# The MLP's up products of an encoder step: pairs of weight blocks multiplied in seven block products instead of eight, each accumulator in a tile of its own, and the norm's rate squared and applied at the down products

## The chip, the cores and the metric

One Trainium2 chip, of which the kernel uses one core. The metric is the device time of one execution in microseconds (us). Before the change it is 2514.52 us, the median of three runs (2514.13 to 2517.27).

## What is computed

The reference is one step of a two-layer encoder on 640 tokens with 1024 features, in float32. The part that the change touches is the end of each layer:

```python
x = x + mix @ w_o
h2 = rmsnorm(x, ln2)
x = x + jnp.square(jax.nn.relu(h2 @ w_up)) @ w_down
```

`w_up` is 1024 x 4096 and `w_down` 4096 x 1024. `rmsnorm` multiplies each token by one number, its rate (the reciprocal root of the mean square), and each feature by a weight of `ln2`. The rate is positive, so `relu(rate * v)**2` is `rate**2 * relu(v)**2`.

## The kernel before, in words

**Layout.** Activations lie with the features on the 128 partitions, so a [1024, 640] activation is a tile of 8 chunks (`k`) of 640 tokens. Tokens are cut in two halves of 320 (`half[0]`, `half[1]`; `HT` is 320). A weight block is 128 output columns by all 1024 inputs, one [128, 1024] tile of 512 KB: `w_up` has 32 blocks, `w_down` 4 x 8.

**Precision.** Every operand is split in two numbers of lower precision, `hi` and `lo` (`split`, lines 132 to 134: ScalarE copies `hi`, then VectorE subtracts to get `lo`). A product is three matmuls, `hi*hi`, `hi*lo` and `lo*hi` (`three`, lines 185 to 194, issued through `mm`, line 80). In the order of a block these are the weight's `hi` with the activation's `hi`, the weight's `hi` with its `lo`, and the weight's `lo` with its `hi`: the third matmul of a block is the first that needs the weight's `lo`. A block is 2 halves x 8 chunks x 3 = 48 matmuls of 128 x 320.

**Weights.** `Feed` (line 136) loads the blocks in a fixed order: `raw` has three buffers, and a load (line 146, on SyncE's queue) starts when the block three places back has been read for the last time. `whi` and `wlo` have two buffers each. `ahead` splits the next block while the one before is in use. The split can only start when TensorE has finished the block that had the buffer before, two places back; with 48 matmuls in each block there is one whole block of time for it. Splits are given priority over other work of their engines by `AHEAD`.

**The MLP** (`mlp`, line 1097). The 4096 inner features come in four groups `b` of 8 blocks. `up(b, ms)` multiplies blocks; `relu2` (lines 1106 to 1111) turns each PSUM result into `gh`, `gl`: VectorE takes relu and rate in one instruction (L1108), ScalarE squares to `gh` (L1109), GpSimd squares again in full precision (L1110), VectorE subtracts for `gl` (L1111). The order is: all of up 0; then for each `b` two blocks of up `b+1`, the 8 blocks of down `b`, and the other six of up `b+1`. A down block is added to `x` by VectorE (L1131, and L1058 in the last group, inside `residual`, which also starts the next norm). TensorE's order is the order of the code; on the other engines a scheduler with priorities orders the instructions.

**PSUM** has eight banks of 512 columns: two pairs `g` (`pair`, line 182) that the blocks take in turn, and two banks each with the tags `c` and `d` (`bank`, line 179).

**The norm before the MLP** is folded in: `residual_raw` (line 1072) makes `Ah`, `Al` from `x * ln2` without the rate while the last product of the attention part runs; `Norm.rate` (line 305) makes the rate beside the first up block, into the tile `nrm.r`.

Of the kernel before, what the change touches and what calls it, by code (L numbers as in the profile page):

```python
# [9 lines left out]
F32 = mybir.dt.float32  # L10
F32R = mybir.dt.float32r
AF = mybir.ActivationFunctionType
ALU = mybir.AluOpType
# [49 lines left out]
def encoder(ctx, tc, xin, wblk, wba, sct, sdelta, prow, pcol, gates, wst, bsr, convw, consts, delta0,  # L63
# [72 lines left out]
    class Feed:  # L136
# [143 lines left out]
    class Norm:  # L280
        def __init__(self, pl, c0, nm, final=False, whole=False):
            self.pl, self.c0, self.nm, self.final = pl, c0, nm, final
            self.r = pl.tile([P, NT], F32, tag="rate", name=f"rate{nm}") if whole else None
            self.acc = pl.tile([P, 2, HT], F32, tag="acc", name=f"acc{nm}")
# [20 lines left out]
        def rate(self, a, wait=3):  # L305
# [21 lines left out]
            nc.scalar.activation(u, pr[:, 0:HT], AF.Copy)  # L327
# [490 lines left out]
    def heads(l, ond, msd, gd, close, norm):  # L818
# [4 lines left out]
        with phase(f"first{l}", 1) as pf:  # L823
# [9 lines left out]
            else:  # L833

                nrm = Norm(pf, 0, "a", whole=True)
# [114 lines left out]
    def merge(l, ond, msd, gd):  # L950
        with phase(f"merge{l}", 1) as pl:
# [99 lines left out]
            es = ExitStack()  # L1051
            nrm = Norm(es.enter_context(phase(f"nb{l}", side="right")), 8 * (2 * l + 1), f"b{l}", whole=True)
            return es, nrm, residual_raw(l, WB_WO, Bh, Bl, f"wo{l}", nrm)

    def residual(l, b0, ah, al, nm, nrm):

        def add(xs, ps, dst, first):
            nc.vector.tensor_tensor(xs, ps[:, :, 0:HT], xs, op=ALU.add)  # L1058
            nrm.add(dst, xs, first, nc.vector if dst == 1 else nc.gpsimd)

        for m in range(4):
            run(gemm(l, b0 + m, ah, al, f"{nm}{m}", lambda ps: add(v2(x[:, m, :]), ps, None, m == 0)))
        with phase(f"g{nm}") as pw:
            g = group(l, range(b0 + 4, b0 + 8), ah, al, nm,
                      lambda i, a, ps: add(x[:, 4 + 2 * i:6 + 2 * i, half[a]], ps, a, False), pw)
            for _ in range(16):
                next(g)
            run(g, fin := nrm.finish(0))
            run(fin)
        return nrm.finish(1)  # L1070
# [26 lines left out]
    def mlp(l, es, nrm, rates):  # L1097
        with phase(f"mlp{l}", 5) as pl:
# [6 lines left out]

            def relu2(ps, hi, lo):
                r = pl.tile([P, 2, HT], F32, tag="r", bufs=3, name=f"r{l}")
                nc.vector.scalar_tensor_tensor(r[:], ps[:, :, 0:HT], 0.0, v2(nrm.r[:]), op0=ALU.max, op1=ALU.mult)  # L1108
                nc.scalar.activation(hi, r[:], AF.Square)  # L1109
                nc.gpsimd.tensor_tensor(r[:], r[:], r[:], op=ALU.mult)  # L1110
                nc.vector.tensor_tensor(lo, r[:], hi.bitcast(F32), op=ALU.subtract)  # L1111
# [6 lines left out]
            up(0, range(KC))  # L1118
            for b in range(FF // D):
                if b + 1 < FF // D:  # L1120
                    up(b + 1, range(2))
                gh, gl = Chunks(tiles, b, 0), Chunks(tiles, b, 1)
                if b + 1 == FF // D:
                    last = l + 1 == DEPTH
                    es.close()
                    es = ExitStack()
                    pn = es.enter_context(phase(f"na{l}", side="right"))
                    return es.close, residual(l, WB_DN + b * KC, gh, gl, f"dn{l}", Norm(pn, 32 if last else 16 * (l + 1), f"a{l}", last))
                for m in range(KC):
                    def add(ps):  # L1130
                        nc.vector.tensor_tensor(v2(x[:, m, :]), ps[:, :, 0:HT], v2(x[:, m, :]), op=ALU.add)  # L1131
                    run(gemm(l, WB_DN + b * KC + m, gh, gl, f"dn{l}{b}{m}", add))
                up(b + 1, range(2, KC))
# [109 lines left out]
```

## Time and profile before

| what | value |
|---|---|
| median of three runs | 2514.52 us |
| the profiled execution's own time | 2513.98 us |
| its span, first to last instruction | 2512.3 us |
| TensorE matmul busy | 2464.4 us (98%) |
| TensorE weight load busy | 2387.2 us (95%) |
| VectorE busy | 1300.4 us (52%) |
| ScalarE busy | 1026.6 us (41%) |
| GpSimd busy | 568.3 us (23%) |
| mean granted TensorE clock | 0.994 |
| up and down products of layer 0 | from 800.5 to about 1261 us |
| up and down products of layer 1 | from about 2040 to 2497 us |

The profile is one execution. PE is TensorE's matmul, PEld its weight load, DVE VectorE, ACT ScalarE, POOL GpSimd, SP SyncE, whose queue issues the loads. A matmul's record lasts longer than the distance to the next one, because matmuls are pipelined: the distance is what counts. Lines such as L133 are lines of the kernel; `whi<-raw` means output `whi`, input `raw`.

### The profile page before, as it was taken

To read this page: it belongs to the slowest core of one execution; us is meant where nothing else is said; L and a number is where in the kernel's file an instruction comes from. 1 tells how busy PE (TensorE), PEld (TensorE's weight loads), DVE (VectorE), ACT (ScalarE), POOL (GpSimd) and SP (SyncE) were. 2 spreads that over 40 slices of the span, in tenths; PEclk is the share of its full clock that TensorE was granted. 3 is DMA by queue.
4 is the path that set the end of the run, shared out by engine and by line. 5 is a ranking of instruction groups with operands and counts; after the bars stand their busy time and mean duration, and the time that the engine had idled before them with its cause. 6 is when DMAs were issued, how large, how long until landed. Compare 5 with 4: busy or idle time off the path is not lost. (4 is left out here: it accounts for less than half of the span.)

```text
span 2512.3 us, 45051 instructions
## 1 busy us (share of the span) xinstructions
PE 2464.4 (98%) x18456; PEld 2387.2 (95%) x18456; DVE 1300.4 (52%) x2686; ACT 1026.6 (41%) x1968; POOL 568.3 (23%) x638
## 2 busy tenths in 40 slices
PE   8999999999999999999999999999999999999998
PEld 7999999998999999999999999999989999999997
DVE  6656776527455433333346677664275553333333
ACT  5767666533123212122347676774322222122122
POOL 0233433211222201011213343331112221011012
PEclk9999999999999999999999999999999999999999
DMA  5233333346532222222233333343564322222221
GB/s 175 83 107 122 103 96 99 115 132 228 167 95 74 72 75 74 76 76 76 85 94 115 102 96 96 101 127 113 164 204 145 92 68 76 76 76 76 73 71 67
DMA packets 124493, 261.28 MB, mean 104 GB/s; under 512 B 17232, under 2 KB 57072, under 8 KB 124288
## 3 DMA queue, kind: packets, MB, share of 16 engines
q1 hardware_dynamic: 123968, 257.10, 32.3%
q8 instruction: 145, 2.38, 0.4%
q0 software_dynamic: 320, 1.31, 0.2%
q14 instruction: 60, 0.49, 0.1%
HBM read 218.22 MB, written 40.15 MB: 103 GB/s over the span
## 5 line engine op out<-in xcount | busy, mean ns | idle before, releaser
L133 ACT ACTIVATE whi<-raw 128x1024 fp32r<-128x1024 f32 x304 | 321.8, 1059 | 1003.9 <-issue 369.6
L134 DVE TENSOR_TENSOR wlo<-raw,whi 128x1024 fp32r<-128x1024 f32 x304 | 397.8, 1309 | 167.8 <-ACT whi L133 153.6
L80 PE MATMUL pg_dn<-gl,whi 128*128 128x320 f32 x1024 | 316.6, 309 | 2.1 <-DVE gl L1111 2.1
L80 PE MATMUL pg_up<-Ah,whi 128*128 128x320 f32 x1024 | 317.1, 310 | 0.0
L80 PE MATMUL pg_dn<-gh,whi 128*128 128x320 f32 x1024 | 316.8, 309 | 0.0
L80 PE MATMUL pg_up<-Ah,wlo 128*128 128x320 f32 x1024 | 316.4, 309 | 0.0
L80 PE MATMUL pg_dn<-gh,wlo 128*128 128x320 f32 x1024 | 316.4, 309 | 0.0
L80 PE MATMUL pg_up<-Al,whi 128*128 128x320 f32 x1024 | 316.4, 309 | 0.0
L80 PE MATMUL pg_g<-Ah,whi 128*128 128x320 f32 x896 | 289.4, 323 | 1.3 <-ACT sg L821 1.3
L80 PE MATMUL pg_g<-Ah,wlo 128*128 128x320 f32 x896 | 276.9, 309 | 0.1
L80 PE MATMUL pg_g<-Al,whi 128*128 128x320 f32 x896 | 276.4, 308 | 0.0
L1110 POOL TENSOR_TENSOR r<-r 128x640 f32<-128x640 f32 x64 | 101.8, 1590 | 684.8 <-ACT gh L1109 684.8
L80 PE MATMUL pg_p<-Ah,whi 128*128 128x320 f32 x768 | 251.4, 327 | 0.0
L80 PE MATMUL pg_p<-Al,whi 128*128 128x320 f32 x768 | 237.0, 309 | 0.4 <-DVE Al L134 0.4
L80 PE MATMUL pg_p<-Ah,wlo 128*128 128x320 f32 x768 | 237.3, 309 | 0.0
L80 PEld LDWEIGHTS pg_dn<-gl,whi 128*128 128x128 f32 x1024 | 192.2, 188 | 2.6 <-DVE gl L1111 2.6
L80 PEld LDWEIGHTS pg_up<-Ah,whi 128*128 128x128 f32 x1024 | 192.2, 188 | 0.0
L80 PEld LDWEIGHTS pg_up<-Al,whi 128*128 128x128 f32 x1024 | 192.2, 188 | 0.0
L80 PEld LDWEIGHTS pg_dn<-gh,whi 128*128 128x128 f32 x1024 | 192.2, 188 | 0.0
L80 PEld LDWEIGHTS pg_dn<-gh,wlo 128*128 128x128 f32 x1024 | 192.2, 188 | 0.0
L80 PEld LDWEIGHTS pg_up<-Ah,wlo 128*128 128x128 f32 x1024 | 192.2, 188 | 0.0
L80 PEld LDWEIGHTS pg_g<-Ah,whi 128*128 128x128 f32 x896 | 168.6, 188 | 9.0 <-issue 3.5
(689 smaller groups left out, 5394.5 us busy)
## 6 DMA issues: line engine op xcount, KB each, us to landing
raw<-in_wblk SPq DMA_DIRECT2D x304, 512.0 KB, 3.6
gd<-sg SPq DMA_DIRECT2D x56, 320.0 KB, 3.5
rg<-gd SPq DMA_DIRECT2D x44, 320.0 KB, 3.3
S<-in_sdelta SPq DMA_DIRECT2D x16, 512.0 KB, 5.7
out<-S SPq DMA_DIRECT2D x16, 512.0 KB, 3.8
gr<-rowd SPq DMA_DIRECT2D x16, 320.0 KB, 5.0
er<-rowd SPq DMA_DIRECT2D x16, 320.0 KB, 4.0
ond<-osb SPq DMA_DIRECT2D x16, 320.0 KB, 2.2
```

Source lines behind the costliest of these rows:

```text
L80: nc.tensor.matmul(out, lhsT=lhsT, rhs=rhs, start=start, stop=stop, **kw)
L133: nc.scalar.activation(dst_hi, src, AF.Copy)
L134: nc.vector.tensor_tensor(dst_lo, src, dst_hi.bitcast(F32), op=ALU.subtract)
L1110: nc.gpsimd.tensor_tensor(r[:], r[:], r[:], op=ALU.mult)
```

## The change

Two neighbouring up blocks, the two halves of the 1024 inputs and the two token halves make a 2 x 2 by 2 x 2 product of blocks: eight products of 12 matmuls (4 chunks x 3). The change computes it in seven, by an identity of the Strassen-Winograd kind.

- `A[k, a]` are the four quarters of the activation (input half `k`, token half `a`). Four sums of them are made once a layer in full precision and split: `S1`, `S2` and `S4` into new tiles, `S3` in place of `A[0, 1]` in `Ah`, `Al`. That takes 16 scaled copies on ScalarE (`scaled`), four sums on VectorE (`plus`) and four splits of 4 x 320 columns. They lie among the first four up blocks of a layer, which are still multiplied the old way.
- `B[k, i]` are the quarters of the two weight blocks (input half `k`, block `i`). Four combinations of them (`s1`, `s2`, 512 columns each) are made by VectorE for each pair, before they are split.
- `seven(b, m)` multiplies blocks `m` and `m+1`. Its weight tiles are `wa` (first raw block: two products), `wb` (the two of `s1`: two products), `wc` (one of `s2` and a quarter of the second raw block: two products) and `wd` (512 columns, the other of `s2`: one product). They take the two buffers of `whi` and `wlo` in turn.
- The accumulators are `Z` (bank `c`), `X` (bank `d`) and `Y` (one bank of a pair). `Z` and `X` are read in the middle of their accumulation (`z1`, `z2`, `x5` are ScalarE copies), and go on accumulating after the read.
- There are 14 such pairs in a layer (two in group 0, four in each of the others), 28 in all. 336 matmuls fewer are issued, which is 28 x 12.
- The rate is no longer applied in the up blocks: `nrm.r` holds its square, and each down block is multiplied by it on VectorE before it is added to `x`, two instructions of 640 columns in place of one (`plus_products`; `residual` takes it as an argument).
- Relu goes to ScalarE. In `seven` ScalarE takes both squares; GpSimd has no instruction there.
- The order of groups stays: pairs `(0, 4)`, `(0, 6)`, `(1, 0)`, eight down blocks, `(1, 2)`, `(1, 4)`, `(1, 6)`, `(2, 0)`, eight down blocks, and so on.

The core of the diff (`Norm` also takes another pool for the rate tile, and `merge` returns three pools instead of one):

```diff
         def parts(self, pl):
-            raw = self.raw.pop(0)
+            self.last = self.raw.pop(0)
+            return self.of(pl, self.last[:])
+
+        def of(self, pl, *src):
             hi = pl.tile([P, D], F32R, tag="whi", bufs=2, name="whi")
             lo = pl.tile([P, D], F32R, tag="wlo", bufs=2, name="wlo")
+            at = 0
             with tc.high_priority(offset=AHEAD):
-                split(hi[:], lo[:], raw[:])
+                for v in src:
+                    n = v.shape[-1]
+                    split(hi[:, at:at + n], lo[:, at:at + n], v)
+                    at += n
             return hi, lo
...
-            nc.scalar.activation(u, pr[:, 0:HT], AF.Copy)
+            nc.scalar.activation(u, pr[:, 0:HT], AF.Copy if self.power == 1 else AF.Square)
...
         def add(xs, ps, dst, first):
-            nc.vector.tensor_tensor(xs, ps[:, :, 0:HT], xs, op=ALU.add)
+            plus(xs, ps, dst)
...
+            def squares(r, hi, lo, eng):
+                nc.scalar.activation(hi, r, AF.Square)
+                if eng is None:
+                    nc.scalar.activation(r, r, AF.Square)
+                else:
+                    eng.tensor_tensor(r, r, r, op=ALU.mult)
+                nc.vector.tensor_tensor(lo, r, hi.bitcast(F32), op=ALU.subtract)
...
             def relu2(ps, hi, lo):
-                r = pl.tile([P, 2, HT], F32, tag="r", bufs=3, name=f"r{l}")
-                nc.vector.scalar_tensor_tensor(r[:], ps[:, :, 0:HT], 0.0, v2(nrm.r[:]), op0=ALU.max, op1=ALU.mult)
-                nc.scalar.activation(hi, r[:], AF.Square)
-                nc.gpsimd.tensor_tensor(r[:], r[:], r[:], op=ALU.mult)
-                nc.vector.tensor_tensor(lo, r[:], hi.bitcast(F32), op=ALU.subtract)
+                r = flat("r", 2)
+                nc.scalar.activation(r[:], ps[:, :, 0:HT], AF.Relu)
+                squares(r[:], hi, lo, nc.gpsimd)
...
-            up(0, range(KC))
+            q, p, sm, u, v = tmp
+            up(0, range(1))
+            scaled(q, 1, 1)
+            scaled(p, 0, 1)
+            plus(sm, p, q)
+            split(*S[1], sm)
+            up(0, range(1, 2))
+            scaled(u, 0, 0)
+            plus(sm, sm, u)
+            split(*S[2], sm)
+            plus(p, p, u)
+            scaled(v, 1, 0)
+            up(0, range(2, 3))
+            plus(sm, sm, v)
+            split(*S[4], sm)
+            up(0, range(3, 4))
+            split(*S[3], p)
...
+            def seven(b, m):
+                gh, gl = dst(b, m)
+                wa = feed.take(l, WB_UP + b * KC + m, ahead=False)
...
+                s1, s2 = (pt.tile([P, 2, 512], F32, tag=t, name=f"{t}{l}{b}{m}") for t in ("t1", "t2"))
+                with tc.high_priority(offset=AHEAD):
...
+                    sub(s1[:, 1, :], B[0, 0], B[0, 1])
+                    neg(s1[:, 0, :], s1[:, 1, :], B[1, 1])
+                wb = feed.of(wp, s1[:].rearrange("p a b -> p (a b)"))
+                Z, X = (bank(t, f"{n}{l}{b}{m}")[:, 0:HT] for n, t in ("zc", "xd"))
+                Y = pair(f"y{l}{b}{m}")[:, 0, 0:HT]
...
+                product(Z, wa, 0, A[0, 0], True)
+                z1 = copy("z1", Z)
+                product(Y, wa, 1, A[1, 0], True)
+                r0, r1 = flat("ra", 2), flat("rb", 2)
+                add(r0[:, 0, :], Y, z1)
+                with tc.high_priority(offset=AHEAD):
+                    sub(s2[:, 0, :], B[1, 1], B[0, 1])
+                    neg(s2[:, 1, :], s1[:, 0, :], B[1, 0])
+                wc = feed.of(wp, s2[:, 0, :], B[1, 1])
+                feed.load()
+                product(Z, wb, 0, S[2], False)
+                z2 = copy("z2", Z)
+                product(X, wb, 1, S[1], True)
+                x5 = copy("x5", X)
+                wd = feed.of(wp, s2[:, 1, :])
+                product(Z, wc, 0, S[3], False)
+                with tc.high_priority(offset=AHEAD):
+                    add(r1[:, 1, :], Z, x5)
+                product(X, wc, 1, S[4], False)
+                add(r0[:, 1, :], X, z2)
+                nc.scalar.activation(r0[:], r0[:], AF.Relu)
+                squares(r0[:], gh[:, :, half[0]], gl[:, :, half[0]], None)
+                feed.ahead()
+                product(Z, wd, 0, A[1, 1], False)
+                nc.scalar.activation(r1[:, 0, :], Z, AF.Relu, scale=-1.0)
+                nc.scalar.activation(r1[:, 1, :], r1[:, 1, :], AF.Relu, scale=-1.0)
+                squares(r1[:], gh[:, :, half[1]], gl[:, :, half[1]], None)
+
+            def plus_products(xs, ps, a):
+                t = flat("t", 2)
+                rate = v2(nrm.r[:]) if a is None else rep(nrm.r[:, half[a]], 1, 2)
+                nc.vector.tensor_tensor(t[:], ps[:, :, 0:HT], rate, op=ALU.mult)
+                nc.vector.tensor_tensor(xs, t[:], xs, op=ALU.add)
```

In the orders below, the changed kernel's L1199 is a matmul of a product, L1204 the copies `z1`, `z2`, `x5`, L1208 the sums with them, L1185 and L1186 the combinations of weights, L1230, L1234 and L1235 relu, L1123 and L1125 the two squares, L1128 the subtraction for `gl`; L133, L134 are the split in both kernels.

ScalarE from the end of one pair to the middle of the next, layer 0. Before, two up blocks there:

```order
L133 ACTIVATE whi<-raw_94_9252 128x1024
L1109 ACTIVATE gh_9308<-r_9365 128x640
L133 ACTIVATE whi<-raw_95_9314 128x1024
L1109 ACTIVATE gh_9308<-r_9425 128x640
L133 ACTIVATE whi<-raw_96_9374 128x1024
```

Now, from the split of the next pair's `wa` (`raw_96`; `t_9633` is the next pair's `s1`, `t_9634` its `s2`, `ra`, `rb` the results of the two token halves):

```order
L133 ACTIVATE whi<-raw_96_9475 128x1024
L1230 ACTIVATE ra_9533<-ra_9533 128x640
L1123 ACTIVATE gh_9494<-ra_9533 128x2x320
L133 ACTIVATE whi<-t_9633 128x1024
L1125 ACTIVATE ra_9533<-ra_9533 128x640
L1234 ACTIVATE rb_9534<-ps_z_9504 128x320
L1204 ACTIVATE z_9656<-ps_z_9641 128x320
L1123 ACTIVATE gh_9494<-rb_9534 128x2x320
L1125 ACTIVATE rb_9534<-rb_9534 128x640
L133 ACTIVATE whi<-t_9634 128x512
L133 ACTIVATE whi<-raw_97_9544 128x512
L1204 ACTIVATE z_9695<-ps_z_9641 128x320
```

Relu and both squares of the pair that ends now stand between the splits of the next pair's first three weight tiles, and the copies of the accumulators stand behind them.

VectorE in the same place. Before, two up blocks:

```order
L1108 SCALAR_TENSOR_TENSOR r_9365<-pg_up_9316,rateb_8518 128x640
L134 TENSOR_TENSOR wlo<-raw_94_9252,whi 128x1024
L1111 TENSOR_TENSOR gl_9309<-r_9365,gh_9308 128x640
L1108 SCALAR_TENSOR_TENSOR r_9425<-pg_up_9376,rateb_8518 128x640
L134 TENSOR_TENSOR wlo<-raw_95_9314,whi 128x1024
```

Now, from the `lo` of a pair's `wa` on:

```order
L134 TENSOR_TENSOR wlo<-raw_94_9295,whi 128x1024
L134 TENSOR_TENSOR wlo<-t_9496,whi 128x1024
L1128 TENSOR_TENSOR gl_9358<-ra_9396,gh_9357 128x2x320
L1208 TENSOR_TENSOR ra_9533<-pg_y_9506,z_9519 128x320
L1185 TENSOR_TENSOR t_9633<-raw_96_9475,raw_97_9544 128x512
L134 TENSOR_TENSOR wlo<-t_9497,whi 128x512
L134 TENSOR_TENSOR wlo<-raw_95_9407,whi 128x512
L1186 SCALAR_TENSOR_TENSOR t_9633<-t_9633,raw_97_9544 128x512
L1128 TENSOR_TENSOR gl_9358<-rb_9397,gh_9357 128x2x320
L134 TENSOR_TENSOR wlo<-t_9497,whi 128x512
L1185 TENSOR_TENSOR t_9634<-raw_97_9544 128x512
L1208 TENSOR_TENSOR rb_9534<-ps_z_9504,x_9572 128x320
```

After these two more stand before the next `wa`: the last combination (L1186, 512 columns) and the sum with `X` (L1208). So there are 14 instructions to a pair where two blocks had six; the combination of the pair after (`t_9633`) stands ahead of the split of this pair's `wc`.

ScalarE at the first pair of a layer, where the sums of activations are split (`S2h`, `S4h`, and `Ah<-s_9049`, which is `S3`; `raw_91` to `raw_93` are blocks 3 to 5; `t_9359` is the first pair's `s1`). Before:

```order
L133 ACTIVATE whi<-raw_91_9042 128x1024
L1109 ACTIVATE gh_9036<-r_9181 128x640
L133 ACTIVATE whi<-raw_92_9130 128x1024
L1109 ACTIVATE gh_9186<-r_9243 128x640
L133 ACTIVATE whi<-raw_93_9192 128x1024
```

Now:

```order
L133 ACTIVATE whi<-raw_92_9158 128x1024
L133 ACTIVATE S2h_9044<-s_9050 128x1280
L1132 ACTIVATE r_9283<-pg_up_9234 128x640
L1123 ACTIVATE gh_9226<-r_9283 128x640
L133 ACTIVATE Ah<-s_9049 128x4x320
L133 ACTIVATE S4h_9046<-s_9050 128x1280
L133 ACTIVATE whi<-t_9359 128x1024
L1132 ACTIVATE r_9346<-pg_up_9297 128x640
L1204 ACTIVATE z_9382<-ps_z_9367 128x320
```

The split of `wb` and the first copy of an accumulator stand behind `S3` and `S4`; `S3` overwrites a part of `Ah` and so waits for the fourth up block's last matmul.

More of the change, by code (lines that the diff above doesn't have):

```diff
@@ L280, in encoder, with __init__ @@
     class Norm:
-        def __init__(self, pl, c0, nm, final=False, whole=False):
-            self.pl, self.c0, self.nm, self.final = pl, c0, nm, final
-            self.r = pl.tile([P, NT], F32, tag="rate", name=f"rate{nm}") if whole else None
+        def __init__(self, pl, c0, nm, final=False, whole=None, power=1):
+            self.pl, self.c0, self.nm, self.final, self.power = pl, c0, nm, final, power
+            self.r = whole.tile([P, NT], F32, tag="rate", name=f"rate{nm}") if whole else None
             self.acc = pl.tile([P, 2, HT], F32, tag="acc", name=f"acc{nm}")
@@ L1116, in up @@
                     run(gemm(l, WB_UP + b * KC + m, Ah, Al, f"up{l}{b}{m}", lambda ps: relu2(ps, hi, lo)), rates)
-            up(0, range(KC))
+            A = {(k, a): [v[:, 4 * k:4 * k + 4, half[a]] for v in (Ah, Al)] for k in range(2) for a in range(2)}
+            S = {i: [psum_pool.tile([P, 4, HT], F32R, name=f"S{i}{t}{l}")[:] for t in "hl"] for i in (1, 2, 4)}
+            S[3] = A[0, 1]
+            tmp = [pl.tile([P, 4, HT], F32, tag=t, name=f"s{i}{l}")[:] for i, t in enumerate(("gh", "gl", "gh", "gl", "gh"))]
@@ new lines, in scaled, with plus @@
+            def scaled(d, k, a):
+                for i in range(4):
+                    c = nrm.c0 + 4 * k + i
+                    nc.scalar.activation(d[:, i, :], x[:, 4 * k + i, half[a]], AF.Copy, scale=col[:, c:c + 1])
+            def plus(d, s0, s1):
+                nc.vector.tensor_tensor(d, s0, s1, op=ALU.add)
+            q, p, sm, u, v = tmp
[4 more added lines that the diff above has]
+            split(*S[1], sm)
@@ L1124, in mlp @@
                     last = l + 1 == DEPTH
-                    es.close()
-                    es = ExitStack()
+                    stacks.pop().close()
+                    stacks.pop().close()
+                    es = stacks.pop()
                     pn = es.enter_context(phase(f"na{l}", side="right"))
-                    return es.close, residual(l, WB_DN + b * KC, gh, gl, f"dn{l}", Norm(pn, 32 if last else 16 * (l + 1), f"a{l}", last))
+                    return es.close, residual(l, WB_DN + b * KC, gh, gl, f"dn{l}", Norm(pn, 32 if last else 16 * (l + 1), f"a{l}", last), plus_products)
                 for m in range(KC):
[L1130 to L1133, printed above, removed]
+                    run(gemm(l, WB_DN + b * KC + m, gh, gl, f"dn{l}{b}{m}", lambda ps: plus_products(v2(x[:, m, :]), ps, None)))
+                for m in (2, 4, 6):
+                    seven(b + 1, m)
     ctx.enter_context(tc.manual_schedule(engines={mybir.EngineType.PE}))
```

41 lines of the change are left out of this document (34 added, 7 removed).

## The prediction

> **What bounds the kernel now.** I read the page first, then the stretches of one layer's MLP, then TensorE's waits. The page's first part gives the shares:
>
> ```profile
> span 2512.3 us, 45051 instructions
> PE 2464.4 (98%) x18456; PEld 2387.2 (95%) x18456; DVE 1300.4 (52%) x2686; ACT 1026.6 (41%) x1968; POOL 568.3 (23%) x638
> ```
>
> TensorE bounds it: busy for 98%. The table by stretches, here one inside the MLP (busy time and count of matmul, weight load, VectorE, ScalarE, GpSimd, then the granted clock), gives the price of a matmul:
>
> ```profile
> 880.00:1000.00 120.00, 120.00 (x820) 120.00 (x819) 41.47 (x42) 23.18 (x25) 12.69 (x8) 1.00 0.24 76
> ```
>
> 820 matmuls in 120 us are 0.1463 us each. A block of 48 takes 7.02, a block product of 12 takes 1.756. VectorE is busy there for 35% and ScalarE for 19%, so they have room, but what counts is when each of their pieces ends. What TensorE waits for now, in the whole run (total, times, longest):
>
> ```profile
> PE pg_pb L80 <- DVE mix L1036: 9.7, 2, 4.9
> ...
> PE ps_msa L80 <- DVE acca L303: 4.5, 2, 2.9
> ...
> PE pg_dn L80 <- DVE gl L1111: 2.1, 2, 1.1
> PE ps_mrb L80 <- DVE dgb L317: 1.9, 2, 1.0
> ```
>
> Inside the MLPs only the last two and a part of the second lie. So fewer matmuls are time, and every new wait of TensorE is time too.
>
> **The change: matmuls removed.** 336 x 0.1463 = 49.2 us. Nothing else on TensorE is added. The border of two blocks costs nothing today (the timeline below has the distance 0.15 across it), so I take the same for a product that starts on another accumulator.
>
> **The change: a wait at the end of each pair.** The next weight tile (`wa` of the next pair, or the first down block) takes the buffer of `wc`, and between `wc` and it lies only `wd`, one product. Before, a whole block of 7.02 lay there. How long a split takes from the release of the buffer is seen at the border from an up to a down block (start, duration, engine):
>
> ```profile
> 987.39 0.31 PE L80 MATMUL pg_dn<-gh,whi 128*128 128x320 f32 x1
> ...
> 987.49 1.06 ACT L133 ACTIVATE whi<-raw 128x1024 fp32r<-128x1024 f32 x1 [5.34 <-issue]
> ...
> 987.59 0.82 DVE L1108 SCALAR_TENSOR_TENSOR r<-pg_up,rateb 128x640 f32<-128x640 f32 x1 [2.85 <-PE pg_up L80]
> ...
> 988.58 1.23 DVE L134 TENSOR_TENSOR wlo<-raw,whi 128x1024 fp32r<-128x1024 f32 x1 [0.17 <-ACT whi L133]
> ```
>
> ScalarE starts 0.10 after the next block's first matmul, takes 1.06, VectorE follows after 0.03 and takes 1.23. What TensorE then needs is seen where it waits for VectorE:
>
> ```profile
> 1201.67 0.31 PE L80 MATMUL pg_dn<-gh,whi 128*128 128x320 f32 x1
> ...
> 1202.15 0.82 DVE L1111 TENSOR_TENSOR gl<-r,gh 128x640 fp32r<-128x640 f32 x1 [1.14 <-POOL r L1110]
> ...
> 1203.03 0.41 PE L80 MATMUL pg_dn<-gl,whi 128*128 128x320 f32 x1 [1.05 <-DVE gl L1111]
> 1203.29 0.31 PE L80 MATMUL pg_dn<-gh,wlo 128*128 128x320 f32 x1
> ```
>
> It starts 0.06 after VectorE's end (1202.97), and the matmul behind it comes 0.26 later instead of 0.15, another 0.11 lost. So `lo` is there 0.10 + 1.06 + 0.03 + 1.23 + 0.06 = 2.48 after `wc` is done, and the first matmul that needs it is due after 12 of `wd` and two of its own, 14 x 0.1463 = 2.05. The wait is 0.43, and with the 0.11 behind it 0.54 us a pair: 28 x 0.54 = 15.1 us. It cannot be less unless ScalarE and VectorE get quicker; it is more if one of them isn't free at that point.
>
> **Are they free?** The durations (mean ns behind the busy time), from the groups by shape; a split's are in the rows above:
>
> ```profile
> L1109 ACT ACTIVATE gh<-r 128x640 fp32r<-128x640 f32 x22 | 16.1, 732 | 0.0
> ...
> L714 DVE TENSOR_TENSOR S<-S,ps_S 128x512 f32<-128x512 f32 x32 | 22.0, 689 | 40.9 <-PE ps_S L80 25.6 <-issue 15.3
> ...
> L1076 DVE TENSOR_TENSOR x<-pg_wo,x 128x320 f32<-128x320 f32 x4 | 1.9, 486 | 4.6 <-PE pg_wo L80 4.6
> ...
> L461 ACT ACTIVATE cb<-pg_p 128x320 f32<-128x320 f32 x48 | 20.1, 419 | 0.0
> ```
>
> and, for a weight block, from issue to landing:
>
> ```profile
> raw<-in_wblk SPq DMA_DIRECT2D x45, 512.0 KB, 3.5
> ```
>
> A pair asks of VectorE two splits of 1024 (1.23), three of 512 and four combinations of 512 (0.69), three sums of 320 (0.49) and two `gl` (0.83): 10.4 us out of 12.3 + 0.54 = 12.8. ScalarE has about 9.8 (512 columns put at 0.62, between the rows for 320 and 640). Both fit, at 81% and 76%, but in order. I walk one pair by the order shown above, with 0 at its first matmul and 0.54 lost in its first product, so that product n ends at 1.756 n + 0.54.
>
> ScalarE: `hi` of `wa` from -1.66 to -0.60; relu and square to 0.86; `hi` of `wb` to 1.92; square to 2.65; relu of `Z` to 3.07; `z1` to 3.49, needed at 4.05. Two squares to 4.95, `wc` to 6.2, `z2` to 6.6, needed at 7.56. `wd` can start at 7.66 and ends at 8.28, `x5` at 8.70, needed at 9.32.
>
> VectorE: `lo` of `wa` to 0.66, of `wb` from 1.95 to 3.18, `gl` to 4.0. Then the sum with `Y`, for which it waits till 4.25 (0.20 after the product's end, as L1108 above), to 4.74. The combination of the pair after, to 5.43: its second raw block was loaded into the buffer that `wa`'s split released at 0.66, and lands 3.5 later at 4.2. `wc` to 6.98, combination 7.67, `gl` 8.50, `wd` 9.19, combination 9.88, sum with `x5` 10.37, relu on ScalarE 10.87. The next `wa` may start at 11.08 + 0.10. So everything is in time, by 0.3 to 0.9 us; the narrowest places are the relu ahead of the next split (0.3), the landing (0.5) and `z1` (0.6). I keep 15.1 us, and 12 (28 x 0.43) to 35 (0.7 more each) as its ends.
>
> **The change: the first pair of a layer.** Beside three up blocks (21.1 us) ScalarE gets 16 scaled copies, four splits of 4 x 320 columns, VectorE four sums and four `lo` of that size. For 1280 columns I extend the line through 640 and 1024: 1.28 on ScalarE and 1.49 on VectorE. The `S3` split may only start when the fourth block is done (T). `hi` of `S3`, `S4` and `wb` then end at T + 1.4, 2.7 and 3.7, a relu (0.73) and `z1` (0.42) at 4.9, where the third product is due at T + 3.5; VectorE's `lo` of the three (1.49, 1.49 and 1.23, from T + 1.4) end at 5.6, where the third matmul of that product is due at 3.8. So 1.9 us are lost if all before is in time, a little less as ScalarE's instructions overlap. It is more where a subtraction meets GpSimd, which squares for `gl` at about that time:
>
> ```profile
> L134 DVE TENSOR_TENSOR Al<-hwo,Ah 128x640 fp32r<-128x640 f32 x7 | 14.5, 2074 | 0.0
> ...
> L134 DVE TENSOR_TENSOR Bl<-mix,Bh 128x640 fp32r<-128x640 f32 x16 | 13.0, 812 | 0.0
> ```
>
> The same subtraction takes 0.81 alone and 2.07 where GpSimd adds squares for the norm meanwhile: 1.3 more where they meet. I take one such meeting in every two layers: 2.5 us a layer, 5.0 in all. The clock may answer to such a wait; at the border of the layers it did:
>
> ```profile
> 1260.00:1266.00 6.00, 3.99 (x25) 3.50 (x26) 4.75 (x7) 4.20 (x7) 0.00 (x0) 1.00 0.29 86
> 1266.00:1271.00 5.00, 5.00 (x26) 5.00 (x26) 0.69 (x2) 0.83 (x2) 0.85 (x1) 0.66 0.28 107
> ```
>
> After 2.0 us without a matmul in 6.0 the clock is 0.66 over 5.0, half a clock for 3.4 us, 1.7 lost. Two layers with a meeting and that fall would be 2 x (1.9 + 1.3 + 1.7) = 9.8; I keep 2 and 9 as ends. The Trainium skill's page "TensorE: Matmul & The Clock Gate", section "What's actually happening", has the clock halve only after an idle window of about 3.4 us; by it this wait would leave the clock alone and the upper end would be 6.4. The row speaks for a fall after less, and the measured row decides.
>
> **The change: down blocks and the ends of the layers.** The multiplication by the rate adds 0.82 to VectorE per down block of 7.02, where 1.23 + 0.83 stand: hidden by the block, except where the next norm waits. At the kernel's end all of it counts, 0.82; between the layers between 0 and two of them, I take 0.8. At the last group's start TensorE waited 1.05 for `gl` (row above), 1.32 with what lies around it (1.36 - 0.15 + 0.11). Now the first token half comes first: relu, both squares and `gl` end at about 4.1, are needed at 1.756 x 1.5 + 0.15 + 0.54 = 3.3, so 0.9 is lost, 0.4 less per layer. Together 0.82 + 0.8 - 0.8 = +0.8; ends -2 and +3. L1108 and GpSimd's squares fall away in the pairs, off the path.
>
> **Sum.** 2513.98 (the profiled execution) - 49.2 + 15.1 + 5.0 + 0.8 = 2485.7. The median is 0.5 above that execution: 2486.2, so 2486 us.
>
> **Rivals.** *The two queues run late* (22%, 2495 to 2509; beyond that 5%, no change). Both engines stand at about 80%, in order, and the walk's margins are 0.3 to 0.6. 20 of the 28 pairs are followed by another pair, where all of the walk's work competes; the other eight run into down blocks, with less beside them. A landing at 5 instead of 3.5, or a few tenths on each instruction, would push relu and the next split by as much: 0.7 us each are 14, 2500; 1.2 us are 24, 2510. For it: VectorE has 2.4 free in 12.8. Against: instructions in a row follow without a gap in the groups above (0.0 idle), and the loads don't meet, since the two of a pair start 6 us apart.
>
> *The clock falls* (7%, slower than before). 28 new short waits of TensorE could make the throttle cut its clock. Where it waited 4.9 us the stretch shows it, and where it waited 1.0 and 1.1 (at the rate and at the last group) it does not:
>
> ```profile
> 625.00:640.00 15.00, 10.13 (x58) 9.90 (x57) 5.88 (x7) 1.06 (x1) 2.77 (x3) 0.77 0.54 190
> ...
> 740.00:1260.00 520.00, 515.27 (x3512) 513.50 (x3510) 206.28 (x213) 124.17 (x151) 83.59 (x53) 1.00 0.24 75
> ```
>
> 0.77 over 15 us is half a clock for about 6.9 us. Half of that in each pair would cost 1.7 us, 28 x 1.7 = 48, so 2534. It decides from 28 us on, which is 1.0 us a pair, or 2.0 us at half clock in 12.8. The Trainium skill's page "TensorE: Matmul & The Clock Gate", section "A second HAM failure mode: psum-queue depth-cycling", says that cycling through PSUM banks with frequent small idle times between groups of matmuls makes the clock swing between half and full. By that rule the forecast would be the 2534 just worked out from rows. The row from 740 to 1260, 1.00 throughout with waits of about 1 us in it, does not bear it out here, and a wait of 0.43 in 12.8 is less.
>
> *Less gain per matmul, or the change does not do what it says.* That 336 matmuls go is in the order of the program. That each still takes 0.1463 could fail where a product waits for a copy in mid-accumulation; 0.05 at each of 196 products would be 10, 2496. It is in the 22%.
>
> *More gain* (3%, below 2478): stalls at 12, first pairs at 2, ends at -2: 2514.5 - 49.2 + 12 + 2 - 2 = 2477.
>
> **Chances and range.** The forecast (2478 to 2495) has 63%. A measurement here can tell about 0.2%, 5 us, from no change: faster 63 + 22 + 3 = 88%, same 5%, slower 7%. The range from 2477 to 2507 leaves out the clock, the no change and the ends of the late queues, some 16%.
>
> **What would show it.** In the changed profile: 336 matmuls fewer at the same distance; in the waits of TensorE about 28 for `wlo` (L134), some 0.4 us each, near 12 in total; a wait of one to three us at the first pair of each layer; none for L1204 elsewhere; granted clock 1.00 in the MLP; VectorE busy for about 80% in stretches of pairs. Waits over 1 us at `wlo`, or many for copies (L1204, L1208), would mean late queues; a clock under 1.00 there, the second rival. The prediction is wrong if a pair takes more than 13.5 or less than 12.6 us.

## The result, and the profile after

The changed kernel takes 2485.19 us (median of four runs), the kernel before 2514.32 us beside it. One of the four was disturbed (3924.99 us, at a granted clock of 0.557): the ratio and all differences below leave it out, and the other three have a median of 2483.95. The ratio is 0.988, with a 95% interval of 0.986 to 0.9899. The profiled execution took 2483.95 us too, 30.0 us less than that of before (2513.98).

The busy times on the page of the changed kernel:

```profile
PE 2424.5 (98%) x18120; PEld 2338.1 (94%) x18120; DVE 1477.9 (60%) x2982; ACT 1212.8 (49%) x2324; POOL 482.1 (19%) x582
```

18120 matmuls are 336 fewer. TensorE still bounds the kernel; VectorE and ScalarE have some 180 and 190 us more to do.

What TensorE waits for, in the whole run of the changed kernel (total, times, longest; the rows that matter here):

```profile
PE ps_z L1199 <- DVE wlo L134: 7.1, 22, 0.9
...
PE ps_msa L80 <- DVE acca L312: 5.1, 2, 3.7
...
PE pg_dn L80 <- DVE wlo L134: 2.1, 8, 0.3
...
PE pg_gf L80 <- DVE Al L134: 1.4, 2, 0.7
...
PE ps_z L1199 <- ACT z L1204: 0.8, 2, 0.4
...
PE pg_dn L80 <- DVE gl L1128: 0.7, 2, 0.3
...
PE ps_msa L80 <- POOL acca L312: 0.4, 2, 0.2
```

The two rows for `wlo` and the one for `z` are new, and so is the last, the next norm's sum in the last down blocks. 22 + 8 = 30 waits: one at the end of each of the 28 pairs, and one in the first pair of each layer. The view counts idle time from the recorded end of the matmul before, and a record lasts 0.31, so it shows less than was lost. One end of a pair in the timeline (start, duration, engine) shows the wait itself; rows of other matmuls and the weight loads are left out:

```profile
1156.48 0.41 PE L1199 MATMUL ps_z<-Ah,wlo 128*128 128x320 f32 x1 [0.26 <-DVE wlo L134]
...
1165.90 0.47 ACT L1235 ACTIVATE rb<-rb 128x320 f32<-128x320 f32 x1 [1.56 <-DVE rb L1208]
...
1166.84 0.31 PE L1199 MATMUL ps_z<-Ah,whi 128*128 128x320 f32 x1
...
1166.94 1.06 ACT L133 ACTIVATE whi<-raw 128x1024 fp32r<-128x1024 f32 x1 [0.57 <-PE ps_x L1199]
...
1167.04 0.49 DVE L1208 TENSOR_TENSOR ra<-ps_x,z 128x320 f32<-128x320 f32 x1 [0.58 <-PE ps_x L1199]
...
1168.04 1.23 DVE L134 TENSOR_TENSOR wlo<-raw,whi 128x1024 fp32r<-128x1024 f32 x1 [0.50 <-ACT whi L133]
...
1168.74 0.31 PE L1199 MATMUL ps_z<-Al,whi 128*128 128x320 f32 x1
...
1169.32 0.41 PE L1199 MATMUL ps_z<-Ah,wlo 128*128 128x320 f32 x1 [0.26 <-DVE wlo L134]
...
1169.57 0.30 PE L1199 MATMUL ps_z<-Ah,whi 128*128 128x320 f32 x1
```

`wd` starts at 1166.84, which releases the buffer; ScalarE starts 0.10 later, VectorE ends at 1169.27, TensorE goes on at 1169.32. That is 0.58 after the matmul before instead of 0.15, so it waited for 0.43, and the next matmul follows after 0.25 (1169.57), another 0.10. From one such wait to the next 12.84 us pass (1156.48 to 1169.32). The row of the split also says that ScalarE had been idle for 0.57 when the buffer came free.

Two stretches of the changed kernel (matmul, weight load, VectorE, ScalarE, GpSimd, clock): two pairs, and most of layer 0's attention end and MLP:

```profile
1048.00:1073.70 25.70, 25.18 (x170) 24.65 (x169) 19.42 (x29) 17.90 (x31) 0.00 (x0) 1.00 0.25 82
...
740.00:1240.00 500.00, 491.03 (x3320) 485.28 (x3319) 291.55 (x355) 213.70 (x323) 39.26 (x25) 1.00 0.24 77
```

VectorE is busy for 76% of the two pairs, ScalarE for 70%, and the clock stayed at 1.00.

The first pair of layer 0 in the timeline of the changed kernel. `S4` is the last of the four sums of activations, `t` the first pair's `s1`, and the fourth up block's first matmul for the quarters that `S3` doesn't touch started at 829.67:

```profile
821.64 1.53 POOL L1127 TENSOR_TENSOR r<-r 128x640 f32<-128x640 f32 x1 [7.51 <-ACT gh L1123]
...
821.97 1.75 DVE L1186 SCALAR_TENSOR_TENSOR t<-t,raw 128x512 f32<-128x512 f32 x1
...
828.32 1.48 DVE L134 TENSOR_TENSOR S2l<-s,S2h 128x1280 fp32r<-128x1280 f32 x1
828.61 2.30 POOL L1127 TENSOR_TENSOR r<-r 128x640 f32<-128x640 f32 x1 [5.43 <-ACT gh L1123]
...
829.83 2.43 DVE L1152 TENSOR_TENSOR s<-s,s 128x1280 f32<-128x1280 f32 x1
829.88 1.28 ACT L133 ACTIVATE Ah<-s 128x1280 fp32r<-128x1280 f32 x1 [1.35 <-PE pg_up L80]
...
831.43 0.31 PE L1199 MATMUL ps_z<-Ah,whi 128*128 128x320 f32 x1
...
832.29 1.28 ACT L133 ACTIVATE S4h<-s 128x1280 fp32r<-128x1280 f32 x1 [1.14 <-DVE s L1152]
...
833.48 1.04 ACT L133 ACTIVATE whi<-t 128x1024 fp32r<-128x1024 f32 x1
...
835.00 0.43 ACT L1204 ACTIVATE z<-ps_z 128x320 f32<-128x320 f32 x1
...
835.48 0.41 PE L1199 MATMUL ps_z<-S2h,whi 128*128 128x320 f32 x1 [0.37 <-ACT z L1204]
...
835.72 1.21 DVE L134 TENSOR_TENSOR wlo<-t,whi 128x1024 fp32r<-128x1024 f32 x1
...
836.99 0.41 PE L1199 MATMUL ps_z<-S2h,wlo 128*128 128x320 f32 x1 [0.95 <-DVE wlo L134]
```

VectorE's last sum took 2.43 beside GpSimd (the sums before it took 1.48), and a combination of weights ahead of it (821.97) took 1.75 instead of the usual 0.69; both are the same in layer 1. ScalarE waited 1.14 for the last sum, and the split of `S4`, that of the first pair's `wb` and the copy `z1` all stand behind each other in its order. TensorE lost 0.63 at `z1` and 1.22 at `wlo`, each with the 0.10 or so on the matmul behind the wait: 1.85 us, and 1.88 in layer 1.

### The profile page after: what moved, and what is told of

It is laid out like the page before. It is cut to its first block, busy times and chain, and to the rows that moved or that the text cites. A ratio compares the mean times of both kernels' runs of the same rounds, so it can differ in the third digit from the quotient of the medians.

```text
span 2482.0 us, 44959 instructions
## 1 busy us (share of the span) xinstructions
PE 2424.5 (98%) x18120; PEld 2338.1 (94%) x18120; DVE 1477.9 (60%) x2982; ACT 1212.8 (49%) x2324; POOL 482.1 (19%) x582
## 5 line engine op out<-in xcount | busy, mean ns | idle before, releaser
L133 ACT ACTIVATE whi<-raw 128x1024 fp32r<-128x1024 f32 (+1 forms) x304 | 309.0, 1018 | 630.6 <-PE pg_dn L80 255.4
L134 DVE TENSOR_TENSOR wlo<-raw,whi 128x1024 fp32r<-128x1024 f32 (+1 forms) x304 | 383.7, 1263 | 171.0 <-ACT whi L133 157.2
L1242 DVE TENSOR_TENSOR t<-pg_dn,rateb 128x640 f32<-128x640 f32 x64 | 52.7, 824 | 202.5 <-PE pg_dn L80 202.5
L80 PEld LDWEIGHTS pg_g<-Al,whi 128*128 128x128 f32 x896 | 168.7, 188 | 1.5
L80 PEld LDWEIGHTS pg_g<-Ah,wlo 128*128 128x128 f32 x896 | 168.2, 188 | 0.0
L479 DVE SCALAR_TENSOR_TENSOR yb<-cb,cw,yb 128x664 f32<-128x664 f32 x144 | 138.1, 959 | 27.4 <-ACT yb L477 25.8
L80 PEld LDWEIGHTS pg_p<-Ah,whi 128*128 128x128 f32 x768 | 145.2, 189 | 6.0 <-issue 2.4
L80 PEld LDWEIGHTS pg_p<-Al,whi 128*128 128x128 f32 x768 | 144.7, 188 | 0.7 <-DVE Al L134 0.7
L80 PEld LDWEIGHTS pg_p<-Ah,wlo 128*128 128x128 f32 x768 | 144.2, 188 | 0.0
```

Source lines behind the costliest of these rows:

```text
L80: nc.tensor.matmul(out, lhsT=lhsT, rhs=rhs, start=start, stop=stop, **kw)
L133: nc.scalar.activation(dst_hi, src, AF.Copy)
L134: nc.vector.tensor_tensor(dst_lo, src, dst_hi.bitcast(F32), op=ALU.subtract)
L479: nc.vector.scalar_tensor_tensor(yb[:, 0:CY], cb[:, j:j + CY], cw[:, c, j:j + 1], yb[:, 0:CY], op0=ALU.mult, op1=ALU.add)
L1242: nc.vector.tensor_tensor(t[:], ps[:, :, 0:HT], rate, op=ALU.mult)
```

## The experiments

Each is an edit of the changed kernel and is measured against the kernel before on the same chip. Differences from the changed kernel are taken from its 2483.95 us.

### The rate and relu alone

All up blocks are whole blocks again; relu on ScalarE, the square of the rate on the down products and the rest stay.

```diff
-            q, p, sm, u, v = tmp
...
-            split(*S[3], p)
+            up(0, range(4))
...
-            seven(0, 4)
-            seven(0, 6)
+            up(0, range(4, KC))
...
-                    seven(b + 1, 0)
+                    up(b + 1, range(2))
...
-                for m in (2, 4, 6):
-                    seven(b + 1, m)
+                up(b + 1, range(2, KC))
```

> The rate's square on the down products, relu on ScalarE and the relay of the rate tile alone; all up blocks stay whole products of 48 matmuls. My theory, that the gain is matmuls removed less the waits they bring, expects no gain: 0.82 more at the kernel's end, 0 to 1 at the border of the layers, and about 0.6 more in each layer's wait for gl at the start of the last down group, because relu now stands behind a weight split on ScalarE; together +1.5 to +3, 2516 to 2517 against 2514.3, which the measurement hardly tells from no change. The rival, that a part of the gain comes from the work taken off VectorE and GpSimd, expects 2500 to 2510.

2516.85 us, ratio 1.001 (1.0001 to 1.0018): this part costs some 3 us (2513.83 before, beside it) and gains nothing. Among its waits the one at the last group's start is longer than before (2.1 there):

```profile
PE pg_dn L80 <- DVE gl L1128: 2.7, 2, 1.3
```

So the whole gain, and a little more, is that of the seven products.

### The last weight tile in a buffer of its own

`wd` no longer takes turns with the others, so the next `wa` takes the buffer of `wb`, and three products lie between them. To make room for it, `x5` uses the buffer of `z1`.

```diff
-        def of(self, pl, *src):
+        def of(self, pl, *src, tag="w", bufs=2, width=D):
...
-            hi = pl.tile([P, D], F32R, tag="whi", bufs=2, name="whi")
+            hi = pl.tile([P, width], F32R, tag=f"{tag}hi", bufs=bufs, name=f"{tag}hi")
...
-                x5 = copy("x5", X)
-                wd = feed.of(wp, s2[:, 1, :])
+                x5 = copy("z1", X)
+                wd = feed.of(pt, s2[:, 1, :], tag="wd", bufs=1, width=512)
```

> The 512 columns of the last weight tile of a pair (wd) get a buffer of their own, so that the next pair's wa takes the buffer of wb, which is released three products earlier. (To make room, the copies z1 and x5 share a tile.) My theory, that the 28 waits of 0.43 for wlo come from the release of wc's buffer one product ahead, expects them gone: 28 x 0.525 = 14.7 us less, 2470.5, and no rows of waiting for wlo over 0.1 us at pair borders but for the first pair of a layer. The rival, that the two queues at about 80% set the pace of a pair, expects the wait to move to copies or splits and the time to stay above 2480.

2470.99 us, ratio 0.9829 (0.9816 to 0.9843), 13 us under the changed kernel; the two MLPs of the profiled executions are 14.2 shorter together. Of the waits for `wlo` only those of the two first pairs are left, and in the stretch of two pairs TensorE is busy all the time:

```profile
PE ps_z L1199 <- ACT z L1204: 3.6, 2, 1.8
...
PE ps_z L1199 <- DVE wlo L134: 0.5, 2, 0.2
```

```profile
1048.00:1072.60 24.60, 24.60 (x170) 24.60 (x169) 18.52 (x28) 17.83 (x32) 0.00 (x0) 1.00 0.29 86
```

The wait at the pairs' ends is the buffer. The first pair waits longer for `z1` here than in the changed kernel (1.8 against 0.4).

### The split in two halves

The buffers stay, but `wa` is split in two times 512 columns, so that the first product can use its half of `lo` earlier.

```diff
+            if self.halves:
+                return self.of(pl, self.last[:, 0:512], self.last[:, 512:1024])
...
+                feed.halves = True
                 feed.ahead()
+                feed.halves = False
```

> Buffers as in the changed kernel; only the split of the tile that follows wd is made in two halves of 512 columns, so that the first product's lo is there earlier: 0.10 + 0.62 + 0.03 + 0.69 + 0.06 = 1.50 after the release, where it is due at 2.05. My theory expects the 28 waits gone, 14.7 us less, 2470.5, as with a buffer apart, for some 0.15 us more on each of the two engines in a pair. The rival of late queues expects no gain or a loss, since each queue gets one instruction more.

2476.11 us, ratio 0.9847 (0.9833 to 0.986): 8 us gained and not 15. The waits for `wlo` at the pairs' ends are gone, but another takes a part of their place. The third product of a pair, in the timeline of this kernel:

```profile
1167.90 0.73 ACT L1125 ACTIVATE gh<-rb 128x640 fp32r<-128x640 f32 x1
...
1168.53 0.42 ACT L1206 ACTIVATE z<-ps_z 128x320 f32<-128x320 f32 x1
...
1168.62 0.31 PE L1201 MATMUL pg_y<-Ah,wlo 128*128 128x320 f32 x1
...
1169.00 0.42 PE L1201 MATMUL ps_z<-S2h,whi 128*128 128x320 f32 x1
```

The copy `z1` (L1206 here) ends at 1168.95, and the third product starts at 1169.00, 0.38 after the matmul before instead of 0.15; 0.35 us are lost with what follows it. This repeats in the pairs that follow a pair, some 20 x 0.35 = 7 us. The two MLPs of the profiled execution are 6.8 shorter than in the changed kernel.

Two things together made `z1` late. The pair starts 0.53 earlier without the wait, and the scheduler put one square more (0.73, the row at 1167.90) ahead of it on ScalarE: three between the split of `wa` and `z1`, where the changed kernel has two. There `z1` ends 1.01 ahead of the third product (1158.80 against 1159.81). In the run before this one the wait is gone too, but the order has two squares, and `z1` ends 0.91 ahead (1153.61 against 1154.52). So the margin was there without the wait; the expectation had not asked what the edit does to the order.

### The first pair without GpSimd

In the four up blocks that are multiplied the old way ScalarE also makes the full square.

```diff
-                squares(r[:], hi, lo, nc.gpsimd)
+                squares(r[:], hi, lo, None)
```

> The full-precision squares of the first four up blocks of a layer go from GpSimd to ScalarE. My theory, that the loss of 1.75 us at the first pair of a layer is the chain of sums and splits, of which the last sum was lengthened from 1.48 to 2.43 us by GpSimd's square beside it, expects that sum at 1.48 and the loss at about 0.9 a layer, 1.7 us less in all, to be read from TensorE's waits and not from the time. The rival, that ScalarE's queue alone sets it, expects the loss to grow, since each of the four blocks adds 0.74 us to ScalarE.

One run, 2483.29 us. The sum takes 1.49 instead of 2.43, and the copy `z1` ends (834.99) well ahead of the third product's first matmul, which starts without a wait (VectorE, ScalarE and TensorE in the timeline of this kernel):

```profile
829.59 1.49 DVE L1152 TENSOR_TENSOR s<-s,s 128x1280 f32<-128x1280 f32 x1
...
834.56 0.43 ACT L1204 ACTIVATE z<-ps_z 128x320 f32<-128x320 f32 x1
...
835.77 0.31 PE L1199 MATMUL ps_z<-S2h,whi 128*128 128x320 f32 x1
```

TensorE then loses 0.1 us in the first pair of layer 0 and 0.3 in that of layer 1, from the distances of its matmuls, instead of 1.85 and 1.88: 3.3 us, more than expected, and the rival (ScalarE's own queue) falls. The combination that took 1.75 takes 0.68 here. One run can't show 3 us in the time; the trace shows where they went.

### Both, as a kernel

> Two edits together: wd in a tile of its own (2470.99 us alone) and, in the four old-way up blocks of a layer, r squared in full precision by ScalarE and not by GpSimd. Theory: the time left at the first pair with wd apart (3.05 us a layer, mostly a wait for z1) comes from VectorE's sums, stretched beside GpSimd, which delay the split of S4 and all that stands behind it on ScalarE. Without GpSimd there some 1.6 us a layer come back, as in the changed kernel: 2467.8 us, 2466 to 2469. Rival: with wd apart it is ScalarE's own queue that is late there (the split of wd is one more piece in it, and the four squares make it longer): 2471 us or more.

2465.3 us, ratio 0.9804 (0.9789 to 0.9818), the fastest of the study, 19 us under the changed kernel. In the MLP's pairs one wait a layer is left, at the first pair:

```profile
PE ps_z L1199 <- DVE wlo L134: 0.6, 2, 0.3
```

It gained more than expected, since with GpSimd gone the first pair of that kernel loses 0.54 and not 1.45. By the distances of the matmuls the first pairs lost 2.8 each with `wd` apart alone, so the 3.05 of the expectation was high too; the two MLPs are 4.4 us shorter than there. The rival (ScalarE's own queue, 2471 or more) falls.

### One VectorE instruction more in a pair

```diff
+                    sub(s2[:, 1, :], s1[:, 0, :], s1[:, 1, :])
                     neg(s2[:, 1, :], s1[:, 0, :], B[1, 0])
```

> One more VectorE instruction of 512 columns (0.69 us) in each pair of the changed kernel, before the last combination; its result is overwritten at once. Theory (the prediction's first rival as a mechanism): what counts is the margin between relu on ScalarE and the next pair's split, measured at 0.23 us. The instruction stands ahead of the sum with X, on which relu waits, so relu and the split come 0.69 - 0.23 = 0.46 later in the 20 pairs that are followed by a pair: 20 x 0.46 = 9 us, 2494.5, with waits for wlo of some 0.9 us there. Rival: VectorE has more than 2 us free in a pair of 12.84, which takes it in: 2485 to 2487.

2487.27 us, ratio 0.989 (0.9875 to 0.9905), 2 to 3 us on top. Most of that is in the first pairs, where the waits for `z1` grew (from 0.8 for both, above) by more than those for `wlo` shrank:

```profile
PE ps_z L1199 <- ACT z L1204: 3.8, 2, 1.9
```

At the ends of the pairs the distances stay at 0.57, but for one of 0.85 between two pairs and one of 0.90 at a down block. The expectation had the wrong sum: relu ahead of the split (L1235, 1165.90 above) waits for the sum of `Z` and `x5`, and the scheduler put the new instruction behind that sum. So this run says that VectorE has room for 0.69 more at that place (it was idle for 0.58 and 0.50 there, in the rows above), but nothing on the margin of ScalarE.

### Three more

Three times the line that was added above.

> Three more VectorE instructions of 512 columns in each pair of the changed kernel. VectorE then has 10.4 + 2.1 = 12.5 us of work in a pair. Each pair followed by a pair should lose 2.07 - 0.23 = 1.8 us more, less where the scheduler puts the sum with X ahead: 20 x 1.0 to 1.8, 2505 to 2522 us, with waits of TensorE of 1.4 to 2.3 us in pairs of 14 us. What it is for is the clock: by the prediction's second rival such waits would make the granted clock fall, by 1.7 us and more a pair on top (2540 or more, clock under 1.00 in stretches of pairs); theory: the clock stays at 1.00.

2491.47 us (two runs, 2488.67 and 2494.27), ratio 0.9909 (0.9889 to 0.9929), some 7 us more, where 20 and more were expected. Two pairs of this kernel by stretch:

```profile
1054.90:1080.70 25.80, 25.16 (x170) 24.64 (x168) 22.97 (x35) 17.85 (x31) 0.00 (x0) 1.00 0.25 82
```

VectorE is busy for 89%, and the distance at the pairs' ends is 0.63 instead of 0.57, 0.06 more. The scheduler put two of the three where VectorE was idle before the sum with `X`. In the first pairs the waits for `z1` are 2.3 us long and those for the sum with `Z` are new, while those for `wlo` are gone. Together the two MLPs are only 4.4 us longer than in the changed kernel. The profiled execution is the slower of the two, and it comes to the first MLP 4.7 later (804.04 against 799.39), by a part that the edit doesn't touch. The waits did not get long enough to tell of the clock what the run was meant to.

### One more with the last tile apart

The same line as in the run with one more, with `wd` in a buffer of its own.

> The same extra VectorE instruction in each pair, but with wd in a tile of its own (2470.99 us without it). A pair takes 12.31 us there and VectorE is then busy for about 90% of it. Theory: not the load counts but that the split of wa has only one product of room; with wd apart it has three products, and 0.46 us more are hidden: 2471 to 2473 us. Rival: at 90% VectorE is the bound or nearly so: 20 x 0.46 = 9 us, 2480.

2480.25 us, ratio 0.9862 (0.9846 to 0.9879): 9 us slower than without the line, the number of the rival and not the theory's. But the place is another one. In the pairs TensorE has no wait at all:

```profile
1048.00:1072.60 24.60, 24.60 (x170) 24.60 (x169) 20.62 (x31) 17.85 (x30) 0.00 (x0) 1.00 0.27 86
```

Nearly all of it is in the first pair of a layer (a wait of some 1 us at one down block of layer 1 is the rest). Its timeline:

```profile
845.61 0.48 DVE L1208 TENSOR_TENSOR ra<-pg_y,z 128x320 f32<-128x320 f32 x1
...
846.21 0.44 ACT L1204 ACTIVATE z<-ps_x 128x320 f32<-128x320 f32 x1 [4.55 <-DVE ra L1208]
...
846.70 0.49 PE L1199 MATMUL ps_x<-S4h,whi 128*128 128x320 f32 x1 [4.10 <-ACT z L1204]
```

and the stretches around that wait (the clock is the number ahead of the DMA share):

```profile
843.50:846.90 3.40, 0.20 (x1) 0.20 (x2) 2.81 (x5) 0.44 (x1) 0.00 (x0) 1.00 0.39 99
846.90:850.30 3.40, 3.40 (x14) 3.40 (x14) 0.41 (x2) 0.82 (x2) 0.00 (x0) 0.50 0.37 139
```

`x5` is copied into the buffer of `z1`, so it waits until VectorE has added `z1` to `Y`; VectorE's late order at the first pair puts that sum behind the splits and combinations of the pair after. TensorE waits 4.10 by the record (a distance of 4.42, since the matmul before started at 842.28) for the copy, and then has half a clock for 3.4 us. So both sides of the expectation were wrong on the place: neither the load of the pairs (84% here) nor their room counts, but a buffer that my own edit had made shared.

### One copy, and two, ahead of relu

These test the margin on ScalarE itself: one copy of a result onto itself ahead of L1235, or two.

```diff
+                nc.scalar.activation(r1[:, 1, :], r1[:, 1, :], AF.Copy)
                 nc.scalar.activation(r1[:, 1, :], r1[:, 1, :], AF.Relu, scale=-1.0)
```

> One more ScalarE instruction of 320 columns (a copy of a result onto itself, 0.42 us and 0.03 to the next) in each pair, right ahead of the relu that stands before the next tile's split on ScalarE. In the changed kernel ScalarE is idle for 0.57 us between that relu and that split in 25 of the 28 pairs (0.23 and none in two others). Theory: it is hidden in the 0.57, so no change but for the places with less room: 2485 to 2486.5 us, waits for wlo as before (gap 0.57). Rival: ScalarE at 76% is late all along its order, and 0.45 show in each pair: 28 x 0.45 = 12.6, 2498.

> Two such copies, 0.90 us. Theory: 0.57 of it are hidden, 0.33 push the split and with it wlo: 28 x 0.33 = 9.2 us, 2494.5 us (2492 to 2498), with gaps of 0.90 for wlo at the ends of the pairs in place of 0.57; the copy z1 stands later in ScalarE's order here and may add a wait of a few tenths. Rival: the queue is elastic and takes that in too: 2485 to 2487.

One: 2483.59 us, ratio 0.9878 (0.9863 to 0.9892), no difference from the changed kernel. Two: 2494.18 us, ratio 0.9915 (0.9899 to 0.9932), 10 more than the changed kernel; in the profiled executions the two MLPs are 9.0 longer together. With one copy, the end of the pair (timeline of that kernel):

```profile
1166.15 0.47 ACT L1235 ACTIVATE rb<-rb 128x320 f32<-128x320 f32 x1 [1.56 <-DVE rb L1208]
...
1166.66 0.47 ACT L1236 ACTIVATE rb<-rb 128x320 f32<-128x320 f32 x1
...
1167.10 0.31 PE L1199 MATMUL ps_z<-Ah,whi 128*128 128x320 f32 x1
1167.15 1.06 ACT L133 ACTIVATE whi<-raw 128x1024 fp32r<-128x1024 f32 x1
```

The idle 0.57 is filled to 0.02, and the split starts no later after `wd`. With two copies it does start later, and the waits grow (waits of that kernel):

```profile
PE ps_z L1199 <- DVE wlo L134: 13.8, 22, 0.9
...
PE pg_dn L80 <- DVE wlo L134: 4.4, 8, 0.6
```

(13.8 + 4.4) - (7.1 + 2.1) = 9.0 us, which is the difference in the MLPs. The margin of the changed kernel is 0.57, and what goes past it shows in every pair.

## Why the prediction was right

Forecast 2486, measured 2485.19 (2483.95 for three of the four runs). By its terms, from the profiled executions:

| term | predicted | measured |
|---|---|---|
| matmuls removed | -49.2 | -49.2 (336 fewer, distance unchanged) |
| wait at the 28 pairs' ends | +15.1 | +14.7 (28 x 0.525) |
| first pairs | +5.0 | +3.7 (1.85 + 1.88) |
| last groups' start | -0.8 | -1.4 (1.32 to 0.60, twice) |
| kernel's end and border of layers | +1.6 | +2.1 (1.5 + 0.6) |
| new waits in down blocks (the next norm's sum) | not in it | +0.9 |
| sum | -28.3 | -29.2 |

The part ahead of the first MLP, where both kernels are the same, came out 1.1 shorter in this execution (799.39 against 800.47). With it the sum is -30.3, and the profiled spans differ by 30.2. From a layer's first up matmul to its last down matmul it was 456.94 in both layers before, and is 441.13 and 441.39 now.

The kernel's end was put at 0.82 and cost 1.5. The distance ahead of its last norm is 3.20 before and 4.06 now, as forecast. The other 0.6 is the clock: in the changed kernel it was halved from 2467.8 on, so the norm's matmuls (from 2469.43) ran at 0.50; before it was halved from 2502.6 on, when the norm's sum (from 2500.28) was done. The border is the rows for `Al`, 0.6 to 1.4, less 0.2 at the norm's sum there. The clock cancels between the two MLPs: before it was halved for 3.4 us at the border (1267.0), which the changed kernel is spared, and in layer 1's attention for 3.4 (1871.1), where the changed kernel has 6.8 (1853.4). That is luck, 1.7 us each way. The row that is not in the forecast is the new wait for `acca` above, 0.34 in each layer, and 0.2 at a down block of layer 1.

*Matmuls.* Right: a product that starts on another accumulator costs nothing, since 7 products and the loss at the end (12.29 + 0.53 = 12.82) are the 12.84 measured, and without the loss two pairs are all TensorE (the second experiment).

*The wait at the pairs' ends.* Right in place, count and size, 0.43 forecast and 0.43 in the rows. The working took four durations from before, and the order of the new work didn't lengthen any. Only the forecast of what the waits' view would show (12 in total) was off: the view counts from the recorded end and shows 0.26 for each.

*The queues.* The walk had relu done 0.3 ahead of the split, the trace 0.5 to 0.6 in 26 of the 28 pairs, 0.2 and none in the others. It set the start of each instruction at the recorded end of the one before, but independent ones start some 0.09 before that end (1166.94 + 1.06 = 1168.00, and the next row of ScalarE starts at 1167.91), so the engines are less full than forecast: 76% and 70%, not 81% and 76%. The first rival (late queues, 22%) was priced rightly as a mechanism: two copies of 0.45 on ScalarE cost 9 us, 28 x (0.90 - 0.57) = 9.2. It did not come since the room was there. The walk's 0.6 for `z1` was 1.0 in the trace. It held without the wait too (the second experiment), and was used up where the halves' order put one square more ahead of it.

*The first pair.* The mechanism was right and the size too large, and that it is off by no more than 1.3 is partly luck, since two steps were wrong and partly cancel. The step "the `S3` split may only start when the fourth block is done" failed, and so does the same statement in the part on the change: `S3` takes the place of the first four chunks of the second token half, which the block's last 12 matmuls don't read, and the split started at 829.88, 1.55 ahead of the first pair's first matmul (831.43). With that, the walk's `lo` of `wb` comes at 5.6 - 1.55 = 4.05 and is needed at 3.8: about 0.25 lost instead of 1.9, and 0.1 and 0.3 are what the run without GpSimd lost. The meeting with GpSimd was forecast once in two layers, at 1.3; it came twice in each layer. It hit the first pair's combination (1.06 longer) and then the last sum (0.95 longer), which stands behind it on VectorE and for which ScalarE waited.

*The clock.* The second rival fell: 28 waits of 0.43 in pairs of 12.84 leave the granted clock at 1.00 in both MLPs, and so do waits of up to 0.9 in the run with two copies. The Trainium skill's page "TensorE: Matmul & The Clock Gate", section "A second HAM failure mode: psum-queue depth-cycling", is not borne out at this size and rate of waits. Its section "What's actually happening", by which the clock halves after an idle window of some 3.4 us, agrees with the run with one more instruction and `wd` apart: after a distance of 4.42 the clock was 0.50 for 3.4 us, and after the first pair's two waits in the changed kernel (0.63 and 1.22 lost) it stayed at 1.00. The border of the layers doesn't fit that rule. Before, the clock was 0.50 from 1267.0 on for 3.4 us, behind distances of 0.51, 0.86 and 1.87 between matmuls, none near 3.4. In the run with the rate alone it did the same behind 1.10, 1.08 and 1.64, and in the changed kernel, behind 1.10, 1.08 and 1.65, it stayed at 1.00. So shorter waits can be enough, and the same waits don't always do it; what decides is not shown. Here the measured rows decide, and not the Trainium skill's rule.

## What to carry to other kernels

When a scheme cuts one step of a ring of two buffers short, the tile two places on is split in the time of that short step: count split latency against the matmuls that lie between release and first use, and give the short tile its own buffer if it doesn't fit, which here was worth 13 to 14 us of 2484. Fit by order, not by load: VectorE at 89% cost a few us, while 0.33 us too many at one place of ScalarE's order cost 9. An edit to one piece can also change the scheduler's order of the others, as the split in halves did. And a buffer that is shared to make room is a new wait, which shows only where the order changes.

## What the runs showed of the hardware

- Some instructions of VectorE take about 1 us longer where GpSimd squares 640 columns beside them: 2.43 instead of 1.49 us for a sum of 1280 columns, 1.75 instead of 0.69 for a combination of 512. Without GpSimd's squares they take 1.49 and 0.68, so it is GpSimd's work that stretches them. But the subtraction for `S2l` (828.32), which was running when the square at 828.61 started, kept its 1.48, and that square took 2.30 where the first of the layer took 1.25. It looks as if the one that starts first runs at full speed and the other waits; no run here tests that.
- At the pairs' ends ScalarE started the split 0.10 us after the first matmul of `wd` where it had been idle (1166.84 to 1166.94), and 0.05 after it where an instruction had ended just before (1167.10 to 1167.15, the run with one copy). The pair's loss there was 0.47 instead of 0.525.
- At the pairs' ends and in the first pairs of the changed kernel the matmul behind one that had waited came at a distance of 0.25 to 0.26 instead of 0.15, whether the distance ahead was 0.57 or 1.26: a tenth on top of each wait.
